# Seven raw weight buffers in a feed-forward, and two feature groups by sevens in every second gate and up block

## The chip, the cores and the metric

The kernel runs on one core of one Trainium2 chip. The core has five engines that work side by side and meet only through semaphores: PE (TensorE, matrix multiplications, with weight loads that overlap them), DVE (VectorE, elementwise work), ACT (ScalarE, activations, casts and copies), POOL (GpSimd, nearly unused here) and SP (SyncE, which issues the DMAs that bring weights from main memory). The metric is the time on the device of one execution, in microseconds, as the median of several runs; smaller is better. All operands are of type float32 or fp32r, the form in which TensorE multiplies them.

## The reference

The reference is a two-layer block on 256 tokens of width 2048. Each layer is a mixer (layer 0: gated delta rule and a linear recurrence; layer 1: two attentions) and a SwiGLU feed-forward with inner width 5632:

```python
def swiglu(hn, w_gate, w_up, w_down):
    return (jax.nn.silu(hn @ w_gate) * (hn @ w_up)) @ w_down

h = h + mixer(rmsnorm(h, norm), ...)
h = h + swiglu(rmsnorm(h, ffn_norm[layer]), ffn_w_gate[layer], ffn_w_up[layer], ffn_w_down[layer])
```

Everything is float32, and the change touches only the two feed-forwards. Their weights are 3 times 2048 x 5632 numbers in each layer, read once.

## The kernel before

**Split products.** A float32 matrix goes through TensorE as two fp32r numbers, a high part (a cast) and the rest. For a weight tile of 128 x 1024 numbers (512 KB), `load` issues a DMA on SP's queue into a buffer `raw`; `split` casts it on ACT (`whi`, L174) and subtracts on DVE (`wlo`, L175). A product then takes three matmuls, high by high, high by low, low by high (`Bank.add`, L366, L367, L368). Both operands are split; the activations are kept as pairs in `X` (features of the normalised state) and `hid` (inner activations).

**Blocks.** The inner width is worked through in eleven gate and up blocks of 512 columns, b = 0 to 10, in three pieces of 4, 4 and 3. After each piece two down blocks (p = 0 and 1) multiply the piece's inner activations by the down weights. `block` does such a block: two column halves `i` (gate and up, or two column groups of the down weights) by two token halves `t` (128 tokens each) make four accumulators F. The contraction is in feature groups `m` of 512; a gate or up block has nd = 4 of them. A group is done in one of two ways.

- *Plain:* four units, each one weight tile, 12 matmuls of 512 columns and one `split`: 48 matmuls.
- *By sevens* (the groups in `comb`): Strassen's scheme in Winograd's form, over the 2 x 2 quarters of the group. Seven products of 6 matmuls each: 42 matmuls. Three of the four weight tiles (b11, b22, b21) are split as they are; four sums of tiles, T1 to T4, are made by `total`: an addition on DVE (`T`, L337), a cast on ACT (`thi`, L340), a subtraction on DVE (`tlo`, L341). The combinations of activations on the other side are made once by `combine` and reused by all blocks. Four of the seven products need sums of their own, M[0] to M[3], in four PSUM banks; `ends` combines them into four tiles e (L413, L415) when the block's last seven is done.

Before the change each block does group 0 by sevens and the others plainly, so a gate or up block has 12 plain units and 7 steps of a seven: 186 matmuls.

**Order.** `block` spreads the steps of the sevens between the plain units: step by step from unit `lead` - 1 on, over `gaps` = units - `lead` - `trail` units. `hooks` put further work ahead of a given unit: `turn` (units 2 and 3) transposes the previous block's result into `hid` on PE (`Ph`, L453), with a cast and a subtraction behind (L455, L456); `combine` is called from hooks too. Program order is the priority; a planner works out ahead of time in which order each engine's queue holds its instructions, and on the chip each queue is worked off in that order.

**Buffers.** `wr` has 3 buffers of 4 KB in each partition for `raw`; in a feed-forward every fourth load goes to one further buffer `raw4`. There are 4 buffers for `whi`, 3 for `wlo`, 3 for `T`, 2 each for `thi` and `tlo`. PSUM has eight banks: four for F, four (`ms`) shared by M[0] to M[3] and the transposes `Ph`. `cf` and `cc4` are temporaries of `combine`, `comb` its result (2 buffers), `fa` the four tiles in which a block's result waits for its `turn`, and `junk` (L281) takes an unused output of the sums of squares after a feed-forward.

The block's way of spreading, before the change:

```python
        sevens = [s for m in comb for s in [seven(m)] for _ in range(7)]
        trail = 3 if nd > 3 else 2
        gaps = max(len(plain) - lead - trail, 1)
...
            while k < len(sevens) and k < (j - lead + 2) * len(sevens) // gaps:
                next(sevens[k])
                k += 1
                if k == len(sevens):
                    e = ends()
```

Of the kernel before, what the change touches and what calls it, by code (L numbers as in the profile page):

```python
# [4 lines left out]
F32, F32R, I32 = dt.float32, dt.float32r, dt.int32  # L5
# [6 lines left out]
T = 256  # L12
# [35 lines left out]
def body(tc, A, out):  # L48
# [13 lines left out]
    mx, ogp = Phase(), Phase()  # L62
    loads, more = [0], []
# [16 lines left out]
    X = res.tile([128, NK, 2, T], F32R, name="X", tag="X")  # L80
# [80 lines left out]
    def load(src):  # L161

        loads[0] += 1
        if more and loads[0] > 0 and loads[0] % 4 == 0:
            raw = mx.tile([128, 1024], F32, name="raw4", tag="raw4", bufs=1)
        else:
            raw = wr.tile([128, 1024], F32, name="raw")
        nc.sync.dma_start(raw, src)
        return raw
# [107 lines left out]

    def sumsq(g, *ts):
        for t in ts or range(2):
            j = mx.tile([128, 512], F32, name="junk", tag="t2", bufs=4)  # L280
            S.activation(j, h[:, t, g * 512:(g + 1) * 512], AF.Square, accum_out=ssp[:, t, g:g + 1])  # L281

    def to_x(g, w, late=False):
# [59 lines left out]

    def combine(x4):

        f = mx.tile([128, 4, T], F32, name="cf", tag="cf", bufs=1)
        c = mx.tile([128, 4, 2, 128], F32, name="cc4", tag="cc4", bufs=1)
        r = mx.tile([128, 2, 4, 2, 128], F32R, name="comb", tag="comb", bufs=2)
        V.tensor_tensor(out=f, in0=x4[:, :, 0].bitcast(F32), in1=x4[:, :, 1].bitcast(F32), op=ALU.add)
        a11, a21, a12, a22 = (f[:, 2 * j:2 * j + 2, t * 128:(t + 1) * 128] for j in range(2) for t in range(2))  # L350
        for i, (x, y) in enumerate(((a21, a22), (a21, a11), (a22, c[:, 1]), (a12, c[:, 2]))):
            V.tensor_tensor(out=c[:, i], in0=x, in1=y, op=ALU.subtract)
        S.copy(r[:, 0], c)
        V.tensor_tensor(out=r[:, 1], in0=c, in1=r[:, 0].bitcast(F32), op=ALU.subtract)
        return r
# [15 lines left out]
    def block(src, x, comb, nd, hooks, tail=0, lead=2):  # L371

        plain = [(i, u) for m in range(nd) if m not in comb for u in (2 * m, 2 * m + 1) for i in range(2)]
        n, ns = len(plain) // 2, len(comb)
        F = [[Bank(acc.tile([128, 512], F32, name=f"F{t}{i}", tag="acc"), n + (ns if t * i == 0 else 0)) for i in range(2)]
             for t in range(2)]  # L380
        M = [Bank(ms([128, 512], f"M{j}"), ns) for j in range(4)]

        def xs(k, t):
            return [x(k)[:, j, t * 128:(t + 1) * 128] for j in range(2)]

        def seven(m):
            c = comb[m]()
            cx = lambda i: lambda kk: [c[:, j, i, kk] for j in range(2)]
            q = lambda j, t: lambda kk: xs(4 * m + 2 * j + kk, t)
            b11 = load(src(0, 2 * m))  # L390
            M[0].add(q(0, 0), split(b11))
            yield
            b12 = load(src(1, 2 * m))
            t, w = total(b11, b12, "T1")
            M[1].add(cx(0), w)
            yield
            b22 = load(src(1, 2 * m + 1))
            F[0][1].add(cx(3), split(b22))
            yield
            M[3].add(cx(1), total(b12, b22, "T3")[1])  # L400
            yield
            t, w = total(t, b22, "T2")
            M[2].add(cx(2), w)
            yield
            b21 = load(src(0, 2 * m + 1))
            F[0][0].add(q(1, 0), split(b21))
            yield
            F[1][0].add(q(1, 1), total(t, b21, "T4")[1])
            yield

        def ends():
            c1, v, w5, w7 = (mx.tile([128, 512], F32, name=f"e{i}", tag=f"e{i}", bufs=1) for i in range(4))
            S.copy(c1, M[0].t)  # L413
            for o, a, b, op in ((v, M[2], c1, ALU.subtract), (w5, M[1], v, ALU.add), (v, M[3], v, ALU.add), (w7, M[3], w5, ALU.add)):
                V.tensor_tensor(out=o, in0=a.t, in1=b, op=op)  # L415
            return [[c1, w5], [v, w7]]

        sevens = [s for m in comb for s in [seven(m)] for _ in range(7)]
        trail = 3 if nd > 3 else 2
        gaps = max(len(plain) - lead - trail, 1)  # L420
        held, e, k = [], None, 0
        for j, (i, u) in enumerate(plain):
            if j in hooks:
                hooks[j]()
            w = unit(src(i, u))
            held.append((i, u, w))
            if j < len(plain) - tail:
                todo, held = [(*held[0], (0, 1))], []
            elif j < len(plain) - 1:
                continue  # L430
            else:
                todo = [(*y, (t,)) for t in range(2) for y in held]
            for i1, u1, w1, tt in todo:
                for t in tt:
                    F[t][i1].add(lambda kk: xs(2 * u1 + kk, t), w1)
            tick()
# [5 lines that stand above are left out]
        return [[y.t for y in f] for f in F], e  # L442

    def ffn(L, then, fin=None):

        gu, dn = A[f"gu{L}"], A[f"dn{L}"]
        todo, cx, ch = [], {}, {}

        def turn():
            hid, j, t, a = todo.pop(0)  # L450
            P = ms([128, 4, 128], "Ph")
            for i in range(4):
                PE.transpose(P[:, i], a[:, i * 128:(i + 1) * 128], tb["ident"])  # L453
            d = hid[:, 4 * j:4 * j + 4, :, t * 128:(t + 1) * 128]
            S.copy(d[:, :, 0], P)  # L455
            V.tensor_tensor(out=d[:, :, 1], in0=P, in1=d[:, :, 0].bitcast(F32), op=ALU.subtract)  # L456

        b = 0
        for piece in (4, 4, 3):
            hid = ogp.tile([128, 16, 2, T], F32R, name="hid", tag="hid")  # L460
            for j in range(piece):
                hooks = {2: turn, 3: turn} if todo else {}
                if b == 0:
                    hooks[4] = lambda: cx.update({0: combine(X[:, 0:4])})
                    hooks[8] = rstd
                if j == 1:
                    hooks[5] = lambda: ch.update({0: combine(hid[:, 0:4])})
                F, e = block(lambda i, u: gu[b, u, i], lambda k: X[:, k], {0: lambda: cx[0]}, 4, hooks, lead=2 if b else 5)
                a = [mx.tile([128, 512], F32, name=f"fa{t}", tag="fa", bufs=4) for t in range(2)]
                for t in range(2):  # L470
                    r = nrm["rs"][:, t:t + 1]
                    V.tensor_tensor(out=a[t], in0=F[t][0], in1=e[t][0], op=(ALU.add, ALU.subtract)[t])
                    S.activation(a[t], a[t], AF.Silu, scale=r)
                for t in range(2):
                    r = nrm["rs"][:, t:t + 1]
                    V.tensor_tensor(out=e[t][1], in0=F[t][1], in1=e[t][1], op=ALU.add)
                    V.scalar_tensor_tensor(out=a[t], in0=e[t][1], scalar=r, in1=a[t], op0=ALU.mult, op1=ALU.mult)
                    todo.append((hid, j, t, a[t]))
                b += 1
            u0 = 2 * (b - piece)  # L480
            for p in range(2):
                end = b == NB and p == 1
                F, e = block(lambda i, u: dn[2 * p + i, u0 + u], lambda k: hid[:, k], {0: lambda: ch[0]}, piece,
                             {2: turn, 3: turn} if todo else {}, 3 if end and fin else 0)
                hs = [[h[:, t, (2 * p + i) * 512:(2 * p + i + 1) * 512] for i in range(2)] for t in range(2)]
                for t in range(2):
                    for i in range(2):
                        V.tensor_tensor(out=e[t][i], in0=hs[t][i], in1=e[t][i], op=ALU.subtract if t > i else ALU.add)
                for t in range(2):
                    for i in range(2):  # L490
                        V.tensor_tensor(out=hs[t][i], in0=F[t][i], in1=e[t][i], op=ALU.add)
                    if end and fin:
                        fin(t)
                if b == NB and not (end and fin):
                    then(2 * p)
                    then(2 * p + 1)
# [687 lines left out]
```

## Time and profile before

| | |
|---|---|
| median of three runs | 2271.32 us (2270.9 to 2272.74) |
| profiled execution | 2270.46 us, its span 2268.7 us |
| PE | 2249.6 us busy, 99% of the span |
| DVE | 1799.9 us busy, 79% |
| ACT | 1217.6 us busy, 54% |
| weights and other data read | 418.22 MB, 185 GB/s over the span |
| feed-forward of layer 0 | about 451 to 1150 us of the span |
| feed-forward of layer 1 | about 1562 to 2262 us of the span |

A row of the page's fifth part is a group of like instructions: line, engine, operation, tile written and tiles read, shapes, count, then the time that they were busy, the mean of one in ns, and the idle time of the engine ahead of them with what ended it. In a timeline each row is an instruction (or several in a row): start, duration, engine, line, and in brackets how long the engine had been idle before it and what it had waited for. Matmuls are pipelined, so the step from one start to the next, not the duration, is what one costs; the same holds, by a little, for DVE. A window row gives the busy time of each engine in a stretch of the span, with counts.

### The profile page before, as it was taken

The page shows a single profiled execution, that of the slowest core. Times are in us where ns is not written, and L with a number is a line of the kernel's source. Part 1 is how long each engine was busy: PE and PEld are TensorE (multiplying, and loading weights), DVE is VectorE, ACT ScalarE, POOL GpSimd, SP SyncE. Part 2 cuts the span into 40 slices and gives each one's busy share as a digit, 9 for nine tenths or more (in the row PEclk, how much of TensorE's full clock was granted, in tenths as well). Part 3 has the DMA queues.
Part 4 walks back from the last instruction along what each step waited for, and adds up shares of the span by engine and source line. Part 5 has one row for each costly group of instructions (what it writes and reads, how often), then busy time and mean ns, then how long its engine had stood idle before and what let it go on. Part 6 is the DMA issues. An engine that isn't in the chain of part 4 may idle for free.

```text
span 2268.7 us, 30176 instructions
## 1 busy us (share of the span) xinstructions
PE 2249.6 (99%) x11146; PEld 1877.4 (83%) x11146; DVE 1799.9 (79%) x2596; ACT 1217.6 (54%) x1631; POOL 2.0 (0%) x6
## 2 busy tenths in 40 slices
PE   8999999999999999999999999999999999999998
PEld 7888888888888888888878888888888888888886
DVE  6899676797887887887976658858887888887888
ACT  7876754564544554454644444445554454554554
POOL 0000000000000000000000000000000000000000
PEclk9999999999999999999999999999999999999999
DMA  7454455666665665666555455566666566566564
GB/s 251 145 176 151 148 153 184 183 203 197 195 204 194 193 202 190 200 199 195 185 166 167 153 168 170 165 188 189 196 207 193 189 202 201 183 203 206 181 218 152
DMA packets 118644, 422.29 MB, mean 186 GB/s; under 512 B 13248, under 2 KB 14784, under 8 KB 118368
## 3 DMA queue, kind: packets, MB, share of 16 engines
q1 hardware_dynamic: 118208, 419.84, 58.8%
q8 instruction: 87, 1.43, 0.3%
q10 hardware_dynamic: 288, 0.52, 0.1%
q14 instruction: 61, 0.50, 0.1%
HBM read 418.22 MB, written 2.10 MB: 185 GB/s over the span
## 4 chain that ended last, share of the span: by engine, by line
PE 94%; DVE 2%; DMA 2%; issue 1%; ACT 0%; SPq 0%; DVEq 0%; ACTq 0%
PE F L366 17%; PE F L367 17%; PE F L368 17%; PE Pw L194 11%; PE Pw L199 6%; PE Px L268 5%; PE Px L270 4%; PE Px L269 4%; PE M L367 3%; PE M L368 3%; PE M L366 2%; PE Ph L453 1%; DVE wlo L175 1%; DMA raw<-in_gu 1%; DMA raw<-in_dn 1%
## 5 line engine op out<-in xcount | busy, mean ns | idle before, releaser
L174 ACT CAST whi<-raw 128x1024 fp32r<-128x1024 f32 x744 | 780.2, 1052 | 874.2 <-PE F L368 373.3
L175 DVE TENSOR_TENSOR wlo<-raw,whi 128x1024 fp32r<-128x1024 f32 x744 | 905.4, 1221 | 331.1 <-PE F L367 129.0
L366 PE MATMUL F<-whi,X 128*128 128x512 f32 x1100 | 431.1, 392 | 0.0
L367 PE MATMUL F<-wlo,X 128*128 128x512 f32 x1100 | 428.3, 389 | 0.0
L368 PE MATMUL F<-whi,X 128*128 128x512 f32 x1100 | 428.2, 389 | 0.0
L194 PE MATMUL Pw<-X,whi 128*128 128x512 f32 x1104 | 398.7, 404 | 1.6 <-ACT whi L174 1.6
L199 PE MATMUL Pw<-X,wlo 128*128 128x256 f32 x1104 | 309.9, 281 | 1.1 <-DVE wlo L175 1.1
L194 PEld LDWEIGHTS Pw<-X,whi 128*128 128x128 f32 x1104 | 208.0, 188 | 51.3 <-ACT whi L174 1.8
L368 PEld LDWEIGHTS F<-whi,X 128*128 128x128 f32 x1100 | 206.5, 188 | 43.2
L367 PEld LDWEIGHTS F<-wlo,X 128*128 128x128 f32 x1100 | 206.7, 188 | 41.8
L366 PEld LDWEIGHTS F<-whi,X 128*128 128x128 f32 x1100 | 206.6, 188 | 41.6
L199 PEld LDWEIGHTS Pw<-X,wlo 128*128 128x128 f32 x1104 | 209.1, 189 | 2.2 <-DVE wlo L175 1.6
L366 PE MATMUL F<-whi,hid 128*128 128x512 f32 x536 | 209.8, 392 | 0.0
L367 PE MATMUL F<-wlo,hid 128*128 128x512 f32 x536 | 208.7, 389 | 0.2 <-DVE wlo L175 0.2
L368 PE MATMUL F<-whi,hid 128*128 128x512 f32 x536 | 208.7, 389 | 0.0
L341 DVE TENSOR_TENSOR tlo<-T,thi 128x1024 fp32r<-128x1024 f32 x136 | 165.8, 1219 | 27.5 <-ACT thi L340 27.4
L340 ACT CAST thi<-T 128x1024 fp32r<-128x1024 f32 x136 | 142.8, 1050 | 34.7 <-DVE T L337 30.3
L367 PEld LDWEIGHTS F<-wlo,hid 128*128 128x128 f32 x536 | 100.7, 188 | 21.0 <-DVE wlo L175 0.6
L368 PEld LDWEIGHTS F<-whi,hid 128*128 128x128 f32 x536 | 100.6, 188 | 20.9
L366 PEld LDWEIGHTS F<-whi,hid 128*128 128x128 f32 x536 | 100.7, 188 | 20.3
L415 DVE TENSOR_TENSOR e<-M,e 128x512 f32<-128x512 f32 x136 | 90.4, 685 | 6.9 <-PE M L368 5.6
L337 DVE TENSOR_TENSOR T<-T,raw 128x1024 f32<-128x1024 f32 x68 | 82.9, 1220 | 5.5 <-DMA raw<-in_gu 3.6
(370 smaller groups left out, 2892.2 us busy)
## 6 DMA issues: line engine op xcount, KB each, us to landing
raw<-in_gu SPq DMA_DIRECT2D x352, 512.0 KB, 4.1
raw<-in_dn SPq DMA_DIRECT2D x176, 512.0 KB, 4.2
raw<-in_w0w SPq DMA_DIRECT2D x74, 512.0 KB, 3.6
raw<-in_wo SPq DMA_DIRECT2D x64, 512.0 KB, 3.6
raw<-in_w1w SPq DMA_DIRECT2D x64, 512.0 KB, 3.6
raw<-in_w1x SPq DMA_DIRECT2D x32, 512.0 KB, 3.7
raw<-in_w0x SPq DMA_DIRECT2D x16, 512.0 KB, 3.6
raw<-in_w0w SPq DMA_DIRECT2D x12, 256.0 KB, 5.1
```

Source lines behind the costliest of these rows:

```text
L174: S.copy(hi, raw)
L175: V.tensor_sub(lo, raw, hi.bitcast(F32))
L194: PE.matmul(P.rearrange("p a b -> p (a b)"), hi[:, kk], X[:, k].rearrange("p a b -> p (a b)"), start=k == 0, stop=False)
L199: PE.matmul(P[:, 0], lo[:, kk], X[:, k, 0], start=False, stop=k == NK - 1)
L268: PE.matmul(Ps[t], x[:, 0, ts], hi[:, kk], start=k == 0, stop=False)
L269: PE.matmul(Ps[t], x[:, 0, ts], lo[:, kk], start=False, stop=False)
L270: PE.matmul(Ps[t], x[:, 1, ts], hi[:, kk], start=False, stop=k == n - 1)
L340: S.copy(hi, t)
L341: V.tensor_sub(lo, t, hi.bitcast(F32))
L366: PE.matmul(self.t, xh, hi[:, kk], start=self.i == kk == 0, stop=False)
L367: PE.matmul(self.t, xh, lo[:, kk], start=False, stop=False)
L368: PE.matmul(self.t, xl, hi[:, kk], start=False, stop=kk == 1 and self.i == self.n - 1)
```

## The change

- **Raw buffers.** `raw4` grows from one buffer to four, used by loads 1, 3, 5 and 6 of every seven, so a feed-forward has seven buffers for weight tiles in place of four.
- **Shared temporaries.** `cf`, `cc4` and, in a feed-forward, `junk` move to the three buffers `T` that `total` uses; `fa` goes from four buffers to two, `comb` from two to three.
- **Two groups by sevens.** Blocks 2, 4, 6, 8 and 10 of each feed-forward do groups 0 and 1 by sevens: 8 plain units and 14 steps, 180 matmuls. Blocks 0, 1, 3, 5, 7 and 9 stay with group 0 alone. M[0] to M[3] and the three accumulators concerned go on over both sevens, and `ends` comes once, after both.
- **Spreading.** With two sevens `trail` is 2, so the 14 steps lie in four gaps: 3 after unit 1, 4 after unit 2, 3 after unit 3 and 4 after unit 4.
- **Combinations.** That of `X`'s second group is made once, in block 1, ahead of unit 8. That of `hid`'s first group, needed by the down blocks, moves in pieces of four from the piece's block j = 1 to its block j = 3; in the piece of three it stays at j = 1.

```diff
-        if more and loads[0] > 0 and loads[0] % 4 == 0:
-            raw = mx.tile([128, 1024], F32, name="raw4", tag="raw4", bufs=1)
+        if more and loads[0] > 0 and loads[0] % 7 in (1, 3, 5, 6):
+            raw = mx.tile([128, 1024], F32, name="raw4", tag="raw4", bufs=4)
...
-            j = mx.tile([128, 512], F32, name="junk", tag="t2", bufs=4)
+            j = (mx.tile([128, 1024], F32, name="junk", tag="T", bufs=3)[:, 0:512] if more else
+                 mx.tile([128, 512], F32, name="junk", tag="t2", bufs=4))
...
-        f = mx.tile([128, 4, T], F32, name="cf", tag="cf", bufs=1)
-        c = mx.tile([128, 4, 2, 128], F32, name="cc4", tag="cc4", bufs=1)
-        r = mx.tile([128, 2, 4, 2, 128], F32R, name="comb", tag="comb", bufs=2)
+        f = mx.tile([128, 4, T], F32, name="cf", tag="T", bufs=3)
+        c = mx.tile([128, 4, 2, 128], F32, name="cc4", tag="T", bufs=3)
+        r = mx.tile([128, 2, 4, 2, 128], F32R, name="comb", tag="comb", bufs=3)
...
-        trail = 3 if nd > 3 else 2
+        trail = 3 if ns == 1 and nd > 3 else 2
...
-                if j == 1:
+                if j == (3 if piece == 4 else 1):
                     hooks[5] = lambda: ch.update({0: combine(hid[:, 0:4])})
-                F, e = block(lambda i, u: gu[b, u, i], lambda k: X[:, k], {0: lambda: cx[0]}, 4, hooks, lead=2 if b else 5)
-                a = [mx.tile([128, 512], F32, name=f"fa{t}", tag="fa", bufs=4) for t in range(2)]
+                if b == 1:
+                    hooks[8] = lambda: cx.update({1: combine(X[:, 4:8])})
+                F, e = block(lambda i, u: gu[b, u, i], lambda k: X[:, k],
+                             {m: lambda m=m: cx[m] for m in range(2 - b % 2 if b else 1)}, 4, hooks, lead=2 if b else 5)
+                a = [mx.tile([128, 512], F32, name=f"fa{t}", tag="fa", bufs=2) for t in range(2)]
```

## The prediction

> **What bounds the kernel now.** I read the page first, then the busy time of single blocks, then the timeline of PE inside a block.
>
> ```profile
> span 2268.7 us, 30176 instructions
> PE 2249.6 (99%) x11146; PEld 1877.4 (83%) x11146; DVE 1799.9 (79%) x2596; ACT 1217.6 (54%) x1631; POOL 2.0 (0%) x6
> PEclk9999999999999999999999999999999999999999
> PE 94%; DVE 2%; DMA 2%; issue 1%; ACT 0%; SPq 0%; DVEq 0%; ACTq 0%
> ```
>
> PE carries 94% of the chain that ended last, at full clock. Inside the feed-forward it is a closed stream:
>
> ```profile
> 599.74 0.39 PE L367 MATMUL F<-tlo,X 128*128 128x512 f32 x1
> ...
> 610.85 0.39 PE L368 MATMUL F<-whi,X 128*128 128x512 f32 x1
> ```
> ```profile
> 531.72 0.60 PE L453 MATMUL Ph<-tab,fa 128*128 128x128 f32 x4
> ...
> 574.79 0.60 PE L453 MATMUL Ph<-tab,fa 128*128 128x128 f32 x4
> ```
>
> The first two rows are 49 matmuls apart: 11.11 / 49 = 0.2267 us each. The other two are the first transposes of blocks 2 and 3: a block takes 43.07 us. It has 186 matmuls; at 0.2266 they are 42.15 us, and the rest, 0.92, is the two turns. So there is no pause, and a matmul left out is worth 0.227 us as long as DVE keeps ahead. How far is DVE from its own limit? The next view gives busy time by block (columns: stretch, its sum, then PE, PEld, DVE, ACT; the stretches run from turn to turn of blocks 1, 2, 4, 5 and 6; 4 follows a down block and has no turn).
>
> ```profile
> 489.00:532.10 43.10, 43.10 (x197) 35.69 (x195) 38.26 (x42) 23.40 (x25) 0.00 (x0) 1.00 0.66 200
> 532.10:575.20 43.10, 43.10 (x197) 35.72 (x195) 34.52 (x36) 22.41 (x25) 0.00 (x0) 1.00 0.63 193
> 703.60:745.70 42.10, 42.10 (x190) 34.89 (x188) 32.74 (x33) 21.14 (x23) 0.00 (x0) 1.00 0.61 197
> 745.70:788.70 43.00, 43.00 (x196) 35.62 (x195) 37.51 (x42) 23.01 (x25) 0.00 (x0) 1.00 0.61 195
> 788.70:831.80 43.10, 43.10 (x198) 35.72 (x196) 34.63 (x36) 22.66 (x25) 0.00 (x0) 1.00 0.62 196
> ```
>
> An ordinary block asks 34.6 us of DVE in 43.1; one with a combination (blocks 1 and 5) about 37.9.
>
> **The change, part by part.**
>
> *Matmuls.* A second group by sevens takes 48 - 42 = 6 matmuls from a block. Five blocks in each of two feed-forwards: 60 x 0.2267 = 13.6 us, all on PE's path. [...]
>
> *DVE's work.* Four splits go, and three splits and four sums come: -4 + 3 + 2 x 4 = 7 more DVE operations of 1024 columns, and -4 + 7 = 3 more casts on ACT.
>
> ```profile
> L174 ACT CAST whi<-raw 128x1024 fp32r<-128x1024 f32 x744 | 780.2, 1052 | 874.2 <-PE F L368 373.3
> L175 DVE TENSOR_TENSOR wlo<-raw,whi 128x1024 fp32r<-128x1024 f32 x744 | 905.4, 1221 | 331.1 <-PE F L367 129.0
> L341 DVE TENSOR_TENSOR tlo<-T,thi 128x1024 fp32r<-128x1024 f32 x136 | 165.8, 1219 | 27.5 <-ACT thi L340 27.4
> ```
> ```profile
> 743.45 1.22 DVE L341 TENSOR_TENSOR tlo<-T,thi 128x1024 fp32r<-128x1024 f32 x1
> 744.58 1.22 DVE L175 TENSOR_TENSOR wlo<-raw,whi 128x1024 fp32r<-128x1024 f32 x1
> 745.72 1.22 DVE L337 TENSOR_TENSOR T<-raw 128x1024 f32<-128x1024 f32 x1
> 746.87 0.69 DVE L456 TENSOR_TENSOR hid<-Ph,hid 128x512 fp32r<-128x512 f32 x1
> 747.48 1.22 DVE L175 TENSOR_TENSOR wlo<-raw,whi 128x1024 fp32r<-128x1024 f32 x1
> ```
>
> Back to back one takes 1.14 us from start to start (0.61 for 512 columns). So an even block asks 34.6 + 7 x 1.14 = 42.6 us of DVE, while PE would need 43.1 - 1.36 = 41.7. ACT, at 22.5 + 3 x 1.05 = 25.6, stays far below. DVE is thus 0.9 us over the block's length, and only its lead can cover that; the next block, with 34.6 to 38 of 43.1, gives it back. The lead, in block 5, where DVE is hardly ever idle for 30 us:
>
> ```profile
> 749.18 1.23 DVE L175 TENSOR_TENSOR wlo<-raw,whi 128x1024 fp32r<-128x1024 f32 x1 [0.49 <-ACT whi L174]
> ...
> 756.26 1.22 DVE L341 TENSOR_TENSOR tlo<-T,thi 128x1024 fp32r<-128x1024 f32 x1
> ...
> 763.75 1.22 DVE L341 TENSOR_TENSOR tlo<-T,thi 128x1024 fp32r<-128x1024 f32 x1
> ```
> ```profile
> 761.38 0.39 PE L367 MATMUL M<-tlo,comb 128*128 128x512 f32 x1
> ...
> 769.54 0.39 PE L367 MATMUL F<-tlo,X 128*128 128x512 f32 x1
> ```
>
> The `tlo` that ends at 757.48 is used at 761.38, the one that ends at 764.97 at 769.54: leads of 3.9 and 4.6 us. I carry 3.9 through an even block. A plain unit costs PE 2.72 and DVE 1.14; a step on a tile 1.36 and 1.14; a step on a sum 1.36 and 2.28; a turn 0.46 and 0.61. From T1 to T3 lie steps 2 and 3, a turn and unit 2: PE 5.9, DVE 5.2, lead 4.6. To T2: 1.36 against 2.28, lead 3.7. To T4: 2.72 against 3.42, lead 3.0. To the second seven's T1: 5.9 against 5.2, 3.7; then 4.6, 3.7 and 3.0 again. So volume alone stops PE nowhere, even if one idle stretch like those below (1.3 to 1.6 us) falls into it.
>
> *A new tight place.* The four steps 4 to 7 of a seven now follow each other with no plain unit between, and `thi` and `tlo` have two buffers each. T4's can only be written when step 4's matmuls are done. With step 4 at 0: its last matmul ends at 5 x 0.227 + 0.39 = 1.5, the cast at 2.6, `tlo` at 3.9; with two handovers, about 4.0. Step 7's first use of `tlo` is at 3 x 1.36 + 0.23 = 4.3. That leaves 0.3 us, and DVE may be inside another operation of up to 1.14. Evenly spread over 0 to 1.14, what exceeds 0.3 averages 0.84 x 0.84 / (2 x 1.14) = 0.31 us. Twice a block: 0.62, and ten blocks: 6.2 us. This is an estimate; the bounds are 0 and 2 x 0.84 x 10 = 16.8. The nearest stall of this kind, in a down block of three groups (seven steps in four gaps):
>
> ```profile
> 2210.47 0.39 PE L366 MATMUL M<-thi,comb 128*128 128x512 f32 x1
> 2211.46 0.50 PE L367 MATMUL M<-tlo,comb 128*128 128x512 f32 x1 [0.61 <-DVE tlo L341]
> ```
>
> Its 0.99 from start to start is 0.76 us over the ordinary step, near one late operation. I take the middle.
>
> *Raw buffers.* Loads per block stay at 16, so SP issues nothing more.
>
> ```profile
> SPq L168 <- DVE wlo L175: 1658.8, 659, 8.7
> ACT whi L174 <- DMA raw<-in_gu: 123.3, 72, 3.7
> ```
> ```profile
> 1100.01 1.05 ACT L174 CAST whi<-raw 128x1024 fp32r<-128x1024 f32 x1 [3.02 <-DMA raw<-in_dn]
> 1102.04 1.23 DVE L341 TENSOR_TENSOR tlo<-T,thi 128x1024 fp32r<-128x1024 f32 x1 [1.28 <-ACT thi L340]
> ```
> ```profile
> 2201.75 1.06 ACT L174 CAST whi<-raw 128x1024 fp32r<-128x1024 f32 x1 [4.50 <-DMA raw<-in_dn]
> 2203.32 0.69 DVE L456 TENSOR_TENSOR hid<-Ph,hid 128x512 fp32r<-128x512 f32 x1 [1.63 <-ACT hid L455]
> ```
>
> SP's queue mostly waits for DVE to free a raw buffer, and ACT in turn for the tile; both DVE pauses come from that: the cast that DVE waits for stood in ACT's queue behind one whose load was late. Three more buffers let loads start earlier. That protects the denser blocks (b12 and b22 are held over several steps). On its own it returns at most stalls like the 0.76 us one; I take 0, bounds -2 and 0.
>
> *Shared temporaries, combinations.* The extra combination costs DVE about 3 us a layer in block 1, which gives the other one away to block 3; both have room (38.3 of 43.1). `cf` and `cc4` in T's buffers make T2 wait for the four small differences, which lie at the head of the same DVE queue; `junk` can make T1 of the last down block wait for four squarings. I take 0, bounds 0 and +4 (one 0.99 us stall at two such places in each layer). `fa` with two buffers: the tiles have been transposed by mid-block, and are rewritten at its end. In an even block all four `ms` banks hold M until `ends`, so the second transposes slip behind unit 4; nobody needs that `hid` before the next block.
>
> *Sum.* 2270.46 - 13.6 + 6.2 = 2263.1 for the profiled execution; the median lies 0.86 above it, so 2264.
>
> **Rivals.**
>
> *DVE becomes the bound of the even blocks (slower).* For it: 42.6 us of work in 41.7, and a queue in fixed order, in which an operation that waits for its cast stops all behind it (the 1.28 us pause above). If the lead is lost early in the block, every pause counts: with one pause 42.6 + 1.3 = 43.9, against 43.1 before, +0.8 a block or 2279; with one in each seven 45.2, +21 us or 2292. It decides from 1.36 us of uncovered time in each even block. Against it: the leads of 3.9 and more, and the unbroken 30 us of block 5. [...]
>
> *Full gain.* If the planner puts a plain unit ahead of step 7, or DVE is free when the cast lands, nothing is lost and a late load or two is saved: 2271.3 - 13.6 - 1 = 2257.
>
> *Nothing moves.* If 0.9 to 1.8 us of each 1.36 come back as stalls, time stays within 0.2%, about 4.5 us, which is what a measurement of this kernel can tell from no change: 2267 to 2276. The saved matmuls would then be there in the trace, and idle PE in their place.
>
> **How the numbers follow.** Stalls of 0.2 to 0.9 us in each even block, 2260 to 2267: 0.42, the forecast's own range. Full gain, 2256 to 2260: 0.18. Nothing moves: 0.15. DVE bound, 2276 and up, about 2283 in the middle: 0.25. Faster is 0.42 + 0.18 = 0.60, same 0.15, slower 0.25. From 2256 to 2280 lies all but about 0.17.
>
> **What would show it.** PE with 60 matmuls fewer; even blocks of 41.7 to 42.7 us and odd ones of 43.1; DVE at 98% or more in even blocks; PE's pauses at the `tlo` of step 7, none elsewhere; fewer waits of ACT for raw tiles. Even blocks longer than 43.1, or pauses at `wlo`, would prove me wrong.

## The result

The changed kernel takes 2253.82 us (median of five runs, 2252.51 to 2256.14), the one before 2271.15 in the same comparison: a ratio of 0.9927, with a 95% interval of 0.9915 to 0.9938. That is 17 us faster, more than double the 7 us that were forecast, and 2 us below the lower end of the range. The execution that was profiled is the slowest of the five, 2256.14 us with a span of 2254.3.

The page of the profile after shows the engines' totals:

```profile
span 2254.3 us, 30168 instructions
PE 2236.5 (99%) x11086; PEld 1866.2 (83%) x11086; DVE 1881.9 (83%) x2678; ACT 1254.9 (56%) x1663; POOL 2.0 (0%) x6
PEclk9999999999999999999999999999999999999999
PE 95%; DMA 2%; DVE 2%; ACT 1%; issue 0%; SPq 0%; DVEq 0%; ACTq 0%
```

60 matmuls are gone (11146 to 11086) and DVE has 82 more instructions: 70 from the second sevens and 12 from two combinations of six instructions each. PE still carries the chain.

Next come the first transposes of block 1 and those of the down block behind block 10, in layer 0. First the kernel before, then the one after:

```profile
488.60 0.49 PE L453 MATMUL Ph<-tab,fa 128*128 128x128 f32 x3
...
1088.07 0.49 PE L453 MATMUL Ph<-tab,fa 128*128 128x128 f32 x3
```
```profile
490.93 0.49 PE L454 MATMUL Ph<-tab,fa 128*128 128x128 f32 x3
...
1083.98 0.49 PE L454 MATMUL Ph<-tab,fa 128*128 128x128 f32 x3
```

This stretch holds the five changed blocks and shrank from 599.47 to 593.05 us, by 6.42. In layer 1 it shrank by 6.47. Five blocks of six matmuls at 0.2267 would be 6.80. So the saved matmuls arrive almost whole: 12.9 of 13.6 us, and the pauses are 0.07 us a block.

The windows from turn to turn of blocks 1, 2 and 3 after the change (columns as in the prediction: PE, PEld, DVE, ACT):

```profile
490.93:536.76 45.83, 45.83 (x207) 37.95 (x206) 43.88 (x48) 25.85 (x27) 0.00 (x0) 1.00 0.65 208
536.76:575.80 39.04, 39.04 (x178) 32.25 (x177) 36.26 (x37) 22.77 (x25) 0.00 (x0) 1.00 0.60 184
575.80:618.88 43.08, 43.08 (x195) 35.70 (x194) 38.51 (x42) 23.89 (x26) 0.00 (x0) 1.00 0.64 204
```

The turn of block 2 now lies behind three steps of the first seven in place of one, so the first window is long by 2.7 and the second short by 4.1; together they are 84.87 against 86.20 before (43.12 + 43.08). DVE is busy 43.88 + 36.26 = 80.1 of these 84.9 us, 94%.

**Where the rest lies.** I cut each span at the first F matmul of a feed-forward and at the first matmul of the mixer behind it, by the timeline of PE. By this cut the feed-forward of layer 0 begins at 437 us before the change, not at about 451.

| us | before | after |
|---|---|---|
| start to the first feed-forward | 437.43 | 439.81 |
| feed-forward, layer 0 | 711.30 | 703.54 |
| mixer, layer 1 | 400.38 | 400.22 |
| feed-forward, layer 1, to the end | 719.56 | 710.77 |

The two feed-forwards together fell by 16.55 us: 12.9 from the stretch above and 3.5 from what follows it, the last down blocks and the ends (60.66 to 59.37 in layer 0, 68.65 to 66.40 in layer 1); the rest, 0.1, lies ahead of it. The first part of the profiled execution came out 2.4 us longer, which hides a part. All of that comes from the first 150 us, 2.0 of it from the first 41 us, in which no instruction was changed. In all fourteen profiles of this study this first part lasts between 436.2 and 440.7 us, with 438.44 and 436.21 for two executions of one and the same program. So I take it for a difference from run to run, and below I compare kernels by the sum of the two feed-forwards as well as by medians: 1430.86 before, 1414.31 after.

### The profile page after: what moved, and what is told of

Its sections match the earlier page's. It is cut to its first block, busy times and chain, and to the rows that moved or that the text cites. A ratio compares the mean times of both kernels' runs of the same rounds, so it can differ in the third digit from the quotient of the medians.

```text
span 2254.3 us, 30168 instructions
## 1 busy us (share of the span) xinstructions
PE 2236.5 (99%) x11086; PEld 1866.2 (83%) x11086; DVE 1881.9 (83%) x2678; ACT 1254.9 (56%) x1663; POOL 2.0 (0%) x6
## 4 chain that ended last, share of the span: by engine, by line
PE 95%; DMA 2%; DVE 2%; ACT 1%; issue 0%; SPq 0%; DVEq 0%; ACTq 0%
PE F L368 16%; PE F L369 16%; PE F L367 16%; PE Pw L194 11%; PE Pw L199 5%; PE Px L268 5%; PE Px L270 5%; PE Px L269 5%; PE M L368 3%; PE M L369 3%; PE M L367 3%; PE Ph L454 1%; DMA raw<-in_gu 1%; DVE wlo L175 1%; PE Psc L992 1%; PE Pt L291 0%
## 5 line engine op out<-in xcount | busy, mean ns | idle before, releaser
L174 ACT CAST whi<-raw 128x1024 fp32r<-128x1024 f32 x734 | 771.1, 1051 | 748.7 <-PE F L369 357.9
L175 DVE TENSOR_TENSOR wlo<-raw,whi 128x1024 fp32r<-128x1024 f32 x734 | 888.8, 1219 | 203.1 <-PE Px L269 68.4
L367 PE MATMUL F<-whi,X 128*128 128x512 f32 x960 | 375.8, 392 | 0.0
L368 PE MATMUL F<-wlo,X 128*128 128x512 f32 x960 | 374.1, 390 | 0.3 <-DVE wlo L175 0.3
L369 PE MATMUL F<-whi,X 128*128 128x512 f32 x960 | 373.7, 389 | 0.0
L342 DVE TENSOR_TENSOR tlo<-T,thi 128x1024 fp32r<-128x1024 f32 x176 | 214.2, 1220 | 43.3 <-ACT thi L341 42.6
L341 ACT CAST thi<-T 128x1024 fp32r<-128x1024 f32 x176 | 185.2, 1053 | 105.9 <-DVE T L338 81.8
L368 PEld LDWEIGHTS F<-wlo,X 128*128 128x128 f32 x960 | 180.3, 188 | 37.6 <-DVE wlo L175 1.2
L369 PEld LDWEIGHTS F<-whi,X 128*128 128x128 f32 x960 | 180.2, 188 | 37.6
L367 PEld LDWEIGHTS F<-whi,X 128*128 128x128 f32 x960 | 180.3, 188 | 36.6
L338 DVE TENSOR_TENSOR T<-raw,raw 128x1024 f32<-128x1024 f32 x74 | 90.1, 1220 | 27.4 <-DMA raw<-in_dn 20.2
L338 DVE TENSOR_TENSOR T<-T,raw 128x1024 f32<-128x1024 f32 x88 | 107.2, 1218 | 4.8 <-DMA raw<-in_dn 4.3
```

What stands on the lines that cost most here:

```text
L174: S.copy(hi, raw)
L175: V.tensor_sub(lo, raw, hi.bitcast(F32))
L338: V.tensor_tensor(out=t, in0=a, in1=b, op=ALU.add)
L341: S.copy(hi, t)
L342: V.tensor_sub(lo, t, hi.bitcast(F32))
L367: PE.matmul(self.t, xh, hi[:, kk], start=self.i == kk == 0, stop=False)
```

## The experiments

All times are medians; "feed-forwards" is the sum of the two in the profiled execution. The kernel before was measured again beside every group of four, at 2271.5, 2271.6 and 2270.0 us, and each ratio is taken to the one beside it.

| kernel | raw buffers | two sevens in | median us | ratio to before (interval) | feed-forwards us |
|---|---|---|---|---|---|
| before | 4 | none | 2271.15 | | 1430.9 |
| changed | 7 | blocks 2, 4, 6, 8, 10 | 2253.82 | 0.9927 (0.9915 to 0.9938) | 1414.3 |
| raw buffers alone | 7 | none | 2267.62 | 0.9985 (0.9976 to 0.9994) | 1427.9 |
| sevens with four | 4 | as changed | 2272.62 | 1.0008 (0.9999 to 1.0018) | 1431.9 |
| five raw buffers | 5 | as changed | 2263.06 | 0.9962 (0.9947 to 0.9977) | 1420.8 |
| six raw buffers | 6 | as changed | 2260.07 | 0.9957 (0.9943 to 0.9970) | 1417.8 |
| two in all | 7 | blocks 2 to 10 | 2249.90 | 0.9910 (0.9893 to 0.9926) | 1409.3 |

### Raw buffers alone, and the sevens without them

The first takes the second seven out of the changed kernel:

```diff
-                if b == 1:
-                    hooks[8] = lambda: cx.update({1: combine(X[:, 4:8])})
-                             {m: lambda m=m: cx[m] for m in range(2 - b % 2 if b else 1)}, 4, hooks, lead=2 if b else 5)
+                             {0: lambda: cx[0]}, 4, hooks, lead=2 if b else 5)
```

> The changed kernel without its second seven: seven raw buffers and shared temporaries stay, every gate and up block does group 0 alone by sevens, and the second group's combination is not made. Theory A (the 14.4 us that the span fell are 60 matmuls, less almost no stall, plus about 3.5 us of late loads that the raw buffers cure in and after the last down blocks): 3.5 us under the kernel before, about 2268, and no PE pause at a tlo in the down blocks of three groups. Theory B (the raw buffers only serve the sevens, the rest is how runs differ): 2271.

Measured: 2267.62 us, and 2.9 us less in the feed-forwards. Theory A holds: the buffers and the shared temporaries alone are worth about 3 to 4 us. The two ends measure 59.35 and 66.88 us, nearly as in the changed kernel.

The second puts the old raw buffers back and keeps the sevens:

```diff
-        if more and loads[0] > 0 and loads[0] % 7 in (1, 3, 5, 6):
-            raw = mx.tile([128, 1024], F32, name="raw4", tag="raw4", bufs=4)
+        if more and loads[0] > 0 and loads[0] % 4 == 0:
+            raw = mx.tile([128, 1024], F32, name="raw4", tag="raw4", bufs=1)
```

> The changed kernel with the old raw buffers: one raw4, every fourth load. Theory A (a load that must wait for a buffer reaches ACT late and DVE behind it): the stalls in the last down blocks return (3.5 us), and even blocks, which hold b12 and b22 over several steps, pause by 0.5 to 1 us each: 2262 to 2268. Rival (loads were never late enough in gate and up blocks): only the 3.5 us, 2257; second rival (raws do nothing): 2254.

Measured: 2272.62 us, beyond even theory A's range. With four raw buffers the saved matmuls are all paid back. Layer 1's end is long again (68.71), layer 0's is not (59.58): that 1.3 us is a part of the change other than the raw buffers, and which part was not separated. PE's timeline in block 2 of this kernel, at step 7 of the first seven:

```profile
543.66 0.39 PE L367 MATMUL F<-whi,X 128*128 128x512 f32 x1
544.55 0.51 PE L368 MATMUL F<-tlo,X 128*128 128x512 f32 x1 [0.50 <-DVE tlo L342]
```

A step of 0.89 from start to start, where the two steps ahead of it took 0.22 and 0.23. Directly ahead of it no load is late. DVE worked without a gap from 523.66 us on, where a sum had waited 0.87 us for its load, and was simply late with `tlo`: its lead was gone. At step 7 of the even blocks DVE stands idle until the cast lands in 18 of 20 places with seven raw buffers, and in 4 of 20 with four. PE's waits for `tlo` (its weight loads, sum in us, times, longest), first of the kernel with four raw buffers, then of the changed one:

```profile
PEld M L368 <- DVE tlo L342: 11.5, 19, 1.4
PEld F L368 <- DVE tlo L342: 7.6, 14, 1.0
```
```profile
PEld M L368 <- DVE tlo L342: 0.8, 2, 0.4
PEld F L368 <- DVE tlo L342: 0.4, 1, 0.4
```

Ahead of DVE stand ACT and the loads. The waits of ACT for weight tiles, first of the kernel with four raw buffers, then of the changed one (sum in us, times, longest):

```profile
ACT whi L174 <- DMA raw<-in_gu: 167.6, 108, 3.7
ACT whi L174 <- DMA raw<-in_dn: 60.1, 34, 5.2
```
```profile
ACT whi L174 <- DMA raw<-in_gu: 6.4, 8, 1.6
```

Before the change they were 123.3 and 57.8 us. They cost PE little as long as DVE was busy 79% of the span: with seven raw buffers and no second seven the gate and up waits are 6.0 us, and the feed-forwards take 2.9 us less than before the change. With the denser blocks four buffers go with the loss of the whole gain (1431.9 us in the feed-forwards against 1414.3), and with seven buffers hardly any of the waits are left in ACT's queue; what remains of late loads is met by DVE's sums (33.7 us in the changed kernel, 10.0 before), and PE loses next to nothing by it (its 0.8 and 0.4 us at `tlo`, above). One thing was not separated: the planner gives each number of buffers another order of the queues. At the pause above, four other matmuls lie between step 7's first product and the one that needs `tlo`, and in the changed kernel none. The runs show what the buffers are worth together with the order that goes with them.

### Five and six raw buffers

```diff
-        if more and loads[0] > 0 and loads[0] % 7 in (1, 3, 5, 6):
-            raw = mx.tile([128, 1024], F32, name="raw4", tag="raw4", bufs=4)
+        if more and loads[0] > 0 and loads[0] % 5 in (1, 3):
+            raw = mx.tile([128, 1024], F32, name="raw4", tag="raw4", bufs=2)
```

> The changed kernel with five raw buffers in place of seven (two raw4, loads 1 and 3 of every five). If late loads are what four raw buffers suffer from (2272.6 with four, 2253.8 with seven), five lie between: 2256 to 2266, with fewer late loads in front of ACT than with four. If one more buffer than before is enough: 2254 to 2256.

For six it reads `% 6 in (1, 3, 5)` and `bufs=3`.

> The changed kernel with six raw buffers (three raw4, loads 1, 3 and 5 of every six). Four gave 2272.6, five 2263.1, seven 2253.8. If each buffer buys about the same: 2258. If six already cover every late load: 2254, with step 7's tlo 0.4 us ahead as with seven.

Measured: 2263.06 and 2260.07 us; the feed-forwards fall 1431.9, 1420.8, 1417.8, 1414.3 with four, five, six and seven. The first buffer buys 11 us, each further one about 3. The kernel with five lies in the expected 2256 to 2266. The median of six lies above the 2258 of the first guess and far above 2254, so seven are not too many.

ACT's waits alone do not account for this: for gate and up tiles they are 40.5 us with five and 6.1 with six, where seven have 6.4. With six the late load stands in DVE's own queue. Ahead of block 2, DVE and then PE:

```profile
518.84 1.23 DVE L338 TENSOR_TENSOR T<-raw,raw 128x1024 f32<-128x1024 f32 x1 [4.14 <-DMA raw<-in_gu]
```
```profile
544.87 0.50 PE L368 MATMUL F<-tlo,X 128*128 128x512 f32 x1 [1.07 <-DVE tlo L342]
```

The sum waited 4.14 us for its load, DVE then worked without a gap up to step 7's `tlo`, and PE stood 1.07 us there: not the 0.4 us of margin that the expectation had for six.

### Two groups by sevens in all blocks

```diff
-                             {m: lambda m=m: cx[m] for m in range(2 - b % 2 if b else 1)}, 4, hooks, lead=2 if b else 5)
+                             {m: lambda m=m: cx[m] for m in range(2 if b > 1 else 1)}, 4, hooks, lead=2 if b else 5)
```

> The changed kernel with two groups by sevens in all blocks from 2 on, not only the even ones: 48 more matmuls saved, 10.9 us on PE. Theory A (an even block overdraws DVE by 0.9 us and its pauses, and the next block gives it back): without a lighter block between, DVE's 42.6 us (45.5 with a combination) and its pauses of 1.3 to 2 set the length, 44 to 46 us a block in place of 41.7 and 43.1: 2275 to 2295, with DVE busy 97% or more there. Rival (DVE is not near its limit): 2243.

Measured: 2249.9 us, neither the 2275 to 2295 of my theory nor the 2243 of the rival. Of the 10.9 us of further matmuls 5.0 arrive in the feed-forwards. Two windows, DVE third: block 6 from its turn to that of block 7, and as long a stretch in block 3 and the down block behind it:

```profile
788.91:830.69 41.78, 41.78 (x190) 34.47 (x188) 40.94 (x42) 25.38 (x27) 0.00 (x0) 1.00 0.62 197
578.87:620.60 41.73, 41.73 (x191) 34.45 (x190) 41.43 (x46) 25.08 (x29) 0.00 (x0) 1.00 0.61 191
```

In the first, the 42 DVE operations of one block with two sevens take 40.94 of 41.78 us, and PE has no idle time. So such a block fits PE's 41.7. My 42.6 was too high. I had added 1.14 us an operation to the busy time of a window, and that counts the tail of each operation in front of an idle stretch (1.22 us long, against 1.14 from start to start). Added up from start to start, the work is 23 x 1.14 + 12 x 0.61 = 33.5 us before and 41.5 after. With a combination it would be 45.1, by an estimate (two more operations of 1.14 and four that start 0.34 apart), and that does not fit. Blocks 3, 7 and 9 have one. In the second window DVE works 41.43 of 41.73 us, 99%, and PE still does not stop, busy 41.73 of 41.73: by this estimate what DVE lacks there comes from its lead and from the lighter down block.

In this kernel the tight place does show. Block 5, step 7 of its second seven, DVE and then PE:

```profile
767.53 1.23 DVE L338 TENSOR_TENSOR T<-raw,raw 128x1024 f32<-128x1024 f32 x1 [1.06 <-DMA raw<-in_gu]
768.68 1.22 DVE L342 TENSOR_TENSOR tlo<-T,thi 128x1024 fp32r<-128x1024 f32 x1
```
```profile
769.00 0.39 PE L367 MATMUL F<-thi,X 128*128 128x512 f32 x1
769.95 0.50 PE L368 MATMUL F<-tlo,X 128*128 128x512 f32 x1 [0.56 <-DVE tlo L342]
```

A sum for the next block stood ahead of `tlo` in DVE's queue and waited 1.06 us for its load; PE lost 0.72 us over the ordinary step. Of the 5.9 us that do not arrive 3.9 are lost between block 1's turn and the one behind block 10, in the two layers together. The other 2.0 lie in layer 1's end (68.43 us against 66.40), and no run separates their cause.

The same program once more, beside the changed one:

> Two groups by sevens in all blocks from 2 on, once more beside the changed kernel: 2250, 3 to 5 us below it if its 48 further matmuls (10.9 us) less pauses of about 6 us hold; level with it if the first difference was that of the runs.

> The changed kernel once more, beside the others: 2254. Its feed-forwards should take 703.5 and 710.8 us again; the first 41 us of the span, in which its first profile was 2 us behind that of the kernel before, should come out differently if that was the difference of runs, and again 2 us late if the change did it.

Measured: 2248.23 us (ratio to before 0.9903, 0.9890 to 0.9917) and 2254.47 (0.9932, 0.9920 to 0.9944). The two intervals do not overlap here: two groups in all blocks is the faster kernel, by 6 us by medians of this pair and by 5.0 and 6.5 in the feed-forwards of its two executions. The changed kernel's feed-forwards sum to 1414.5 again. Its first part was 440.10 us this time, so this execution alone does not say whether the change did it; the spread over all profiles, and the 2.2 us between the two executions of the other program, are what speaks for the run.

### More work for DVE

In the changed kernel, the weight subtraction of the first three plain units of each even block is done twice, with the same result; then that of the first six (`j < 6`).

```diff
-            w = unit(src(i, u))
+            raw = load(src(i, u))
+            w = split(raw)
+            if ns == 2 and j < 3:
+                V.tensor_sub(w[1], raw, w[0].bitcast(F32))
```

> The changed kernel with three idle repeats of the weight subtraction in each even block (plain units 0 to 2; the result is the same): 3.4 us more DVE, 46 in 41.7. Theory A (lead of about 3.9 us, deficit 4.3 and pauses of 1 to 2): 1 to 2.5 us of PE pause in each even block, 2264 to 2279. Rival 1 (DVE sets the length of even blocks already): 3.4 x 10 = 34 us, 2288. Rival 2 (the lead is much larger): 2254.

> The changed kernel with six idle repeats of the weight subtraction in each even block (plain units 0 to 5): 6.8 us more DVE, about 48.4 in 41.7, and about 84 in the 84.8 of a pair of blocks. If the lead pools over two blocks, most is still covered: the three repeats cost 0.35 us a block, six should cost 1.5 to 3 a block, 2267 to 2285. If each further operation now shows in full, 0.35 + 3.4 a block: 2291.

Measured: 2257.30 and 2266.54 us (ratios 0.9945, 0.9930 to 0.9960, and 0.9977, 0.9968 to 0.9986). In the feed-forwards three repeats cost 3.2 us, 0.32 per even block for 3.4 us of work; six cost 12.7, 1.27 for 6.8. Neither theory's number is met: three cost less than theory A's 1 to 2.5, six a little less than its 1.5 to 3. So the first three operations are nearly free and the next three cost 0.95 of 3.4. About 5.5 of the 6.8 us of extra work do not show in the time, which I put down to DVE's lead and the lighter block behind; DVE does not set the length of the even block.

### A third buffer for the sums

`thi` and `tlo` get three buffers each, which five raw buffers pay for.

```diff
-        hi = mx.tile([128, 1024], F32R, name="thi", tag="thi", bufs=2)
-        lo = mx.tile([128, 1024], F32R, name="tlo", tag="tlo", bufs=2)
+        hi = mx.tile([128, 1024], F32R, name="thi", tag="thi", bufs=3)
+        lo = mx.tile([128, 1024], F32R, name="tlo", tag="tlo", bufs=3)
```

> The changed kernel with three buffers for thi and tlo in place of two, paid for with two raw4 (five raw buffers). Theory (step 7's tlo has 0.4 us to spare because DVE stands idle at the head of its queue until the cast lands, 0.67 and 1.44 us in an even block): with a third buffer that tlo comes over 1 us ahead of its use, and DVE's idle time ahead of it goes, but PE gains nothing: the same time as with five raw buffers and two of each, within 2 us. Rival (the two buffers cost PE time that the trace spreads elsewhere): 3 us or more below it.

Measured: 2258.39 us (0.9942, 0.9928 to 0.9957), 4.7 below five raw buffers with two of each. By medians that is the rival's "3 us or more"; but the intervals overlap, and of the 5.4 us between the two spans 3.4 lie ahead of the first feed-forward. In the feed-forwards the difference is 1.9 us, within the theory's 2. So the runs do not decide between the two. What the third buffer does can be seen in block 2, DVE and PE:

```profile
538.27 1.22 DVE L342 TENSOR_TENSOR tlo<-T,thi 128x1024 fp32r<-128x1024 f32 x1
```
```profile
541.93 0.39 PE L368 MATMUL F<-tlo,X 128*128 128x512 f32 x1
```

Step 7's `tlo` is done at 539.49, 2.4 us ahead of its use, and DVE did not wait for it.

Two more mixtures were measured. With four raw buffers and three for the sums:

> The changed kernel with four raw buffers and three buffers each for thi and tlo. With four raw buffers and two of these the saved matmuls came back as pauses (2272.6); with five, the third buffer bought 4.7 us. Theory (a late load becomes a PE pause where a sum's two buffers leave 0.4 us): a good part of it goes, 2262 to 2268. Rival (late loads stop PE on their own): 2270 or more.

2271.84 us (1.0006, 0.9997 to 1.0015), feed-forwards 1433.0: the theory falls and the rival's time holds. With four raw buffers PE stops at `tlo` whether the sums have two buffers or three: its weight loads wait 11.5 us (M) and 7.6 us (F) with two, 13.2 and 6.3 us with three. And two sevens in all blocks, with five raw buffers and three for the sums:

> Two groups by sevens in all blocks from 2 on (2249.9), with three buffers for thi and tlo and five raw buffers. There step 7's tlo ends 0.05 us ahead of its use and PE pauses by 0.2 to 0.7 us at it. Theory (these pauses come from the two buffers and a DVE that no longer stands idle): they go, worth 3 to 5 us, if five raw buffers are enough: 2245 to 2248. Rival (late loads with five raw buffers cost more): above 2250.

2259.15 us (0.9946, 0.9930 to 0.9963), feed-forwards 1418.2: the rival again. Here two raw buffers are worth more than a third buffer for the sums, by 8.9 us in the feed-forwards (1409.3 against 1418.2).

## Why the prediction was wrong

Its direction and its main term were right, and the time came out below the range. For the profiled execution the sum was 2263.1 us and 2256.14 was measured.

- **Matmuls, 13.6 us.** Right: 12.9 us arrive in the changed blocks.
- **A new tight place, 6.2 us of pauses.** This is the step that failed. The chain itself was right. In block 2, ACT, DVE and PE of the changed kernel:

```profile
541.50 1.05 ACT L341 CAST thi<-T 128x1024 fp32r<-128x1024 f32 x1 [0.31 <-PE M L369]
```
```profile
542.59 1.22 DVE L342 TENSOR_TENSOR tlo<-T,thi 128x1024 fp32r<-128x1024 f32 x1 [0.67 <-ACT thi L341]
...
558.08 1.22 DVE L342 TENSOR_TENSOR tlo<-T,thi 128x1024 fp32r<-128x1024 f32 x1 [1.44 <-ACT thi L341]
```
```profile
544.25 0.39 PE L368 MATMUL F<-tlo,X 128*128 128x512 f32 x1
```

  The cast starts when step 4's matmuls are done, `tlo` ends at 543.81 and is used at 544.25: 0.44 us to spare where I had worked out 0.3. Wrong was what I put beside it, that DVE would be inside another operation when the cast lands, at random. DVE stands idle at the head of its queue for 0.67 us, and in the block's second seven for 1.44, until the cast is there, and so it starts at once. The same holds at 18 of the 20 places in the ten even blocks, with 0.39 to 0.44 us to spare; at the other two, in block 10, DVE comes from another operation and 0.29 us are left. So what DVE does when the cast lands is not random here. The price falls on DVE's spare time and not on PE: 0.7 us of pauses in all ten blocks instead of 6.2. In the kernel with two sevens everywhere, where DVE waits 16.8 us in all for `thi` and not 42.6 as in the changed one, pauses at this place do come (0.1 to 0.9 us, six of them in the first execution).
- **Raw buffers, taken as 0 with a bound of -2.** Too small, and too lightly reasoned. Alone with the shared temporaries they bring 3 to 4 us. More than that, they carry the whole gain: with four of them the sevens bring nothing. I had written that they protect the denser blocks, and gave that no price. It is 14 us: from block 1's turn to the one behind block 10 the two layers take 1200.3 us with four buffers and 1186.1 with seven.
- **DVE's work, 42.6 in 41.7.** Mis-sized by about 1 us; 41.5 by starts. DVE was to be busy 98% or more in even blocks, and is 93% in block 2's window (36.26 of 39.04). The ledger of leads gave 3.0 us as the smallest (step 7 aside), and 3.4 us of extra work cost 0.32, which fits it.
- **Shared temporaries, 0.** Not seen to cost anything; layer 0's end even became 1.3 us shorter with a cause that was not settled.
- **The rival "full gain", 2257.** It is what happened, and by its second condition: DVE is free when the cast lands. Its case was given 0.18, and its own price still left out 2.5 us of late loads. The slower rival, DVE bound, did not come: DVE has room for about three more operations in an even block (three cost 0.32 us).
- **The profiled execution against the median.** 2.4 us in the first part of the span, and 2.3 us between the profiled run and the median, I take for differences of runs. They moved the median below the range; by its profiled execution alone the kernel would have lain just inside it.

So the corrected sum is 2270.5 - 12.9 - 3.5 - 0.3 + 2.4 = 2256.2 (0.3 for the mixer and what lies ahead of block 1's turn), against 2256.14 measured.

## What to carry to other kernels

When a change makes a helper engine's work denser, ask first for the waits that were free until now: the loads that came late 109 times (72 and 37 waits of ACT) while DVE was busy 79% of the span were almost harmless, and with the same four buffers they went with the loss of the whole gain (2272.62 us) once the changed blocks held more work for DVE, busy 94% in blocks 1 and 2 of the changed kernel. A deeper prefetch and a denser schedule can each be worth little alone and much together (here 3 to 4 us, nothing, and 17), so measure each without the other and both together. And in a planned queue, do not price a tight handover as if the partner were busy at random: look whether the order leaves it idle there, as it did here at 18 of 20 places, and ask how much idle time it has left to give.

## What was not expected of the hardware

The time up to the first feed-forward differed by up to 4.5 us (436.2 to 440.7) between profiled executions whose instructions there do the same work, and by 2.2 us between two executions of one program; the stages behind it repeated to 0.1 us in the changed kernel (703.54 and 703.57, 710.77 and 710.89), and to 1.0 and 0.4 us in the kernel with two sevens in all blocks (700.5 and 699.5, 708.9 and 708.5). For differences of a few us, the sum of the stages that a change touches says more than the time of the whole, down to some 1.5 us for both feed-forwards.
